# Two more Strassen products joined over two quarters, transposed spreads, a stacked rotary key and four-head value blocks in a two-layer encoder trunk

## The chip, the cores and the metric

The kernel runs on one core of a Trainium2 chip. The metric is device time in microseconds of one execution; a time given for a kernel is the median of several runs. A profile is one further execution, recorded by the hardware profiler. Engines are named as in the profile: PE (TensorE, matrix products), PEld (its weight loads), DVE (VectorE), ACT (ScalarE), POOL (GpSimd), SP (SyncE, which mainly issues DMAs).

## The reference

Input and output are 512 tokens of 1024 float32 features. Two layers work on a residual stream `h`. Between them one shared set of keys and values is computed.

```python
# layer 0
hn = rms_norm(h, mix_pre_g[0])
m  = conformer_conv(hn, ...)              # 1024->2048, gate, 31 taps, layer_norm, silu, 1024->1024
h  = h + rms_norm(m, mix_post_g[0])
f  = square(relu(rms_norm(h, ffn_pre_g[0]) @ w1)) @ w2    # 1024 -> 4096 -> 1024
h  = h + rms_norm(f, ffn_post_g[0])
# keys and values for layer 1
hn     = rms_norm(h, kv_in_g)
c_kv   = rms_norm(hn @ w_dkv, kv_norm_g)          # 256 wide
k_rope = apply_rope(hn @ w_kr, cos, sin)          # 64 wide, shared by the 8 heads
k_nope = c_kv @ w_uk                              # 8 heads x 128
v      = c_kv @ w_uv                              # 8 heads x 128
# layer 1
q  = rms_norm(rms_norm(h, mix_pre_g[1]) @ w_dq, q_norm_g) @ w_uq   # 8 x (128 + 64 rotary)
m  = attention(q, k_nope, k_rope, v, block-causal mask of 64 tokens) @ w_o
h  = h + rms_norm(m, mix_post_g[1])
f  = square(relu(rms_norm(h, ffn_pre_g[1]) @ w1)) @ w2
out = h + rms_norm(f, ffn_post_g[1])
```

## The kernel before

**Arithmetic.** A float32 operand `x` is held as two tiles of TensorE's fp32r type: `hi`, a ScalarE copy of `x`, and `lo = x - hi`, a VectorE subtraction. `split` makes the pair. A product is three fp32r products: hi by hi, lo by hi, hi by lo.

**A program that writes its own order.** `trunk` issues nothing directly. It records operations in a `Program`. `due` works backward and gives each one a latest time; `schedule` places them greedily on the engines, with modelled costs and, for DMAs, a modelled landing (`arrival`); `replay` runs the resulting order against a finer model of the DMA queues. `run` repeats due, schedule and replay 16 times, keeps the order with the shortest replayed span, and issues it. All instructions are issued from one line, L790, so the profile's groups differ by tile names and shapes and not by line. Where the schedule leaves TensorE empty, `schedule` adds filler products of the identity with itself (`mm<-ident` and `bc<-ident` in the profile).

**Tiles.** `big` is a pool of 49 tiles of 128x512 in SBUF. `tmp` has five more; `raw` (8) receives weights of 128x1024; `wh` (5) and `wl` (6) hold a weight's hi and lo parts; `mm` (6) and `bc` (2) are PSUM banks of 128x512; `stat` tiles hold a few numbers per token.

**Feed-forward.** The 4096 hidden features are taken in four quarters `q`. The first two use a Winograd form for the first matrix. In the third and fourth (`q` = 2 and 3) the block `ff1` computes eight products of 128 hidden features by 512 tokens, and ScalarE squares the rectified result into `Z`. The second matrix `ff2` is applied with Strassen's seven products over 2x2 blocks (token halves by hidden halves, hidden halves by output halves). Each of the seven is 24 products of 512 columns on TensorE: two halves `u` of the inner dimension, two token blocks `i`, two 128-wide slices and the three hi/lo combinations. `terms(p)` forms the left side (a difference of two `Z` blocks for products 1, 2, 5, 6 and 7) and splits it. `weight` forms the right side: a plain load on SP's queue, plus for products 3, 4, 6 and 7 an accumulating load on POOL's queue, or for product 1 a second plain load and a VectorE subtraction; then a split. `collect` adds a finished product to the accumulators, in the fourth quarter to every output block that it serves. After the third quarter the accumulators of the seven products are combined into the four output blocks.

Products 2 and 6 (`TOGETHER`) of the third quarter are not run there. Their left sides are kept as pairs, and they run at the end of the fourth quarter, into the same PSUM tiles as the fourth quarter's own products 2 and 6. The order `PRODUCTS` of the others is

```python
TOGETHER = (2, 6)
PRODUCTS = ((3, 6, 2, 1, 4, 5, 7),) * 2 + ((3, 1, 4, 5, 7), (3, 5, 1, 4, 7))
```

As output blocks become complete, `post_norm` takes them: square sums, the norm, the addition to `h`. In layer 0 it does so for tokens in two halves (`HA`, token blocks 0 and 1; `HB`, 2 and 3), and `prenorm` then transposes the half for the next layer on TensorE (`bc<-ident,h`). In layer 1 `finish` stores each token block in two halves, one from SP's queue and one from ScalarE's.

**Spreads.** `spread` turns a column of one number per token (`r`, in a `stat` tile) into a tile with that number along a row, the same in all 128 partitions: one float32 product of `r` broadcast with the identity per 128 tokens. There are four such blocks after the first norm, eight in the conv module's layer norm, four for the norm ahead of the keys (`r1`) and four in the key latents. `row_sums` multiplies by a constant matrix (`bc<-col,...`).

**Keys, queries, values.** For each half of the tokens, `latent` computes `c_kv` (2 x 24 products of 256 columns), then come the rotary key (`products(("kr",), ...)`, 24 products of 256 columns, its 64 columns twice side by side), `rotate` and two of the query latent's three blocks. The weights of `dkv`, `kr` and `dq` pass through `scaled`, which multiplies by a gain and splits. Then `project(u)` runs the up-projections listed in `PROJECTIONS` for the units `u` = -1 to 15, two per head, between the scores and the softmax of the heads. `values(pr)` makes the values of two heads: four token blocks of six products of 256 columns each.

Of the kernel before, what the change touches and what calls it, by code (L numbers as in the profile page):

```python
# [14 lines left out]
P = 128  # L15
# [21 lines left out]
for _name, _w in (  # L37
# [11 lines left out]


PROJECTIONS = {
    -1: (("uqr", 0), ("uq", 0), ("uq", 1), ("uk", 0), ("uk", 1), ("uv", 0)),
    0: (("uqr", 1),),
    1: (("uk", 2), ("uq", 2)),
    2: (("uv", 1),),
    3: (("uk", 3), ("uq", 3), ("uqr", 2)),
    5: (("uk", 4), ("uq", 4)),
    6: (("uv", 2),),
    7: (("uk", 5), ("uq", 5), ("uqr", 3)),
    9: (("uk", 6), ("uq", 6)),  # L60
    10: (("uv", 3),),
    11: (("uk", 7), ("uq", 7)),
}


# [11 lines left out]
}  # L77


TOGETHER = (2, 6)  # L80
PRODUCTS = ((3, 6, 2, 1, 4, 5, 7),) * 2 + ((3, 1, 4, 5, 7), (3, 5, 1, 4, 7))


BLK = {}
# [12 lines left out]
ATT = ("uq", "uqr", "uk", "uv", "wo")  # L97

GAINS = {"dq": "mix_pre1", "dkv": "kvin_g", "kr": "kvin_g"}


def _blk(name, cols=1024):
# [43 lines left out]
def _ff(layer):  # L146
    for q in EARLY:
        _first(layer, q)
    for q in range(4):
        for m in range(8 if q not in EARLY else 0):  # L150
            _blk(("ff1", layer, q, m))
        for dh in range(2):
            for ku in range(4):
                _blk(("ff2", layer, q, dh, ku))
                USE.pop()
        for r, p in [(q, p) for p in PRODUCTS[q]] + [(r, p) for r in (2, 3) for p in TOGETHER if q == 3]:
# [12 lines left out]
    _blk(("dq", _m))  # L169
for _u in range(-1, 16):  # L170
    for _key in PROJECTIONS.get(_u, ()):
        _blk(_key, {"uv": 512, "uqr": 384, "uq": 384, "uk": 256}[_key[0]])
_out("wo")
_ff(1)
NBLK = len(_cols)
# [108 lines left out]

BESIDE = 3000.0

FILL = 222.0

SLACK = 500.0
# [35 lines left out]
class Program:  # L325
# [14 lines left out]

    def record(self, *ways):
        op = Op(len(self.ops))
        op.early = self.early
# [96 lines left out]
        op.flight = 1500.0 + op.load + (3500.0 if slow > 1 else 0.0)  # L440

    def arrival(self, op, end, state):

        if "dma" not in op.method:
# [310 lines left out]
    def run(self, tags, rounds=16):  # L755
# [8 lines left out]
        for _ in range(rounds):  # L764
            self.due(start)
            span, start, sequence = self.schedule(tags)
            spans = [self.replay(sequence, pace) for pace in PACES]
# [26 lines left out]
def trunk(ctx: ExitStack, tc: tile.TileContext, xT, xN, wts, vec, along, rope, cw, out):  # L794
# [81 lines left out]
    def scaled(name, src):  # L876

        lo, hi = ([big(F32R) for _ in range(2)] for _ in range(2))
        for o in range(2):
# [153 lines left out]
    def spread(r, t0, n, dst=None, tag=BC):  # L1033

        bc = nc.tile(tag)
        for b in range(n // P):
            nc.tensor.matmul(
                bc[:, b * P : (b + 1) * P], lhsT=r[:, b : b + 1].to_broadcast([P, P]), rhs=ident, start=True, stop=True
            )
        if dst is not None:  # L1040
            nc.scalar.activation(dst[:, t0 : t0 + n], bc[:, :n], AF.Copy)
        return bc
# [219 lines left out]
    def feed_forward(layer, X, F):  # L1262
# [11 lines left out]
        for q in range(4):  # L1274
# [5 lines left out]
            for m in range(8 if q not in early else 0):  # L1280
# [3 lines left out]
                for th in range(2):  # L1284
# [4 lines left out]
            def terms(p):  # L1289

                left, A = STRASSEN[p][0], []
                for u in range(2):
                    src = Z[left[0][0]][u]
                    if len(left) > 1:
                        d = tmp()
                        nc.vector.tensor_tensor(out=d, in0=src, in1=Z[left[1][0]][u], op=ALU.subtract)
                        src = d
                    A.append(pair())
                    split(src, slice(0, T), A[u])
                return A  # L1300

            def sides(q, p):
                return [weight(("ff2", layer, q, p, u)) for u in range(2)]
# [31 lines left out]
                return b, to[1]  # L1335

            steps = [(u, i) for u in range(2) for i in range(2)]
            for p in PRODUCTS[q]:
                A = terms(p)
                collect(p, product({}, A, sides(q, p), steps))  # L1340
                if q == 3 and p in (5, 7):
                    for i in range(2):
                        yield done((0, int(p == 5)), i)
            if q > 1:
                for p in TOGETHER:
                    both[q, p] = terms(p)
            if q == 3:

                pts = {p: product({}, both[2, p], sides(2, p), steps, last=False) for p in TOGETHER}
                w = {p: sides(3, p) for p in TOGETHER}  # L1350
                for i in range(2):
                    for p in TOGETHER:
                        product(pts[p], both[3, p], w[p], [(0, i), (1, i)], first=False)
                        collect(p, {i: pts[p][i]})
                        yield done((1, int(p == 6)), i)
            if q == 2:

                for to, p in quad.items():
# [409 lines left out]
    def values(pr):  # L1768

        hi, lo = weight(("uv", pr))  # L1770
        V[pr] = [pair() for _ in range(2)]
        for tb in range(4):
            pt = nc.tile(MM)
            ts = slice(tb * P, (tb + 1) * P)
            for k in range(2):
                ws = slice(k * 256, (k + 1) * 256)
                for j, (a, b) in enumerate(((CKV[k][0], hi), (CKV[k][0], lo), (CKV[k][1], hi))):
                    nc.tensor.matmul(
                        pt[:, :256], lhsT=a[:, ts], rhs=b[:, ws],
                        start=(k == 0 and j == 0), stop=(k == 1 and j == 2),  # L1780
                    )
# [63 lines left out]
    def attend(hd, PT):  # L1845
        po = nc.tile(MM)
        seq = []
        for j, (n, o) in enumerate(((0, 0), (1, 0), (2, 0), (2, 2 * P))):
            vo = 256 * (j % 2) + 128 * (hd % 2)
            for a, b in ((0, 0), (0, 1), (1, 0)):  # L1850
                seq.append((j * P, V[hd // 2][j // 2][a][:, vo : vo + P], PT[n][b][:, o : o + T - j * P]))

        seq = seq[:1] + seq[3:] + seq[1:3]
        for n, (q0, a, b) in enumerate(seq):
# [47 lines left out]
def _layout(i):  # L1902
# [33 lines left out]
    put(("kr",), _tiles(np.concatenate([i["kv_w_kr"]] * 2, axis=1), slice(None)))  # L1936
    uq = i["mla_w_uq"][0].reshape(384, NH, 192)
    for p in range(4):
        put(("uv", p), _tiles(i["kv_w_uv"], slice(256 * p, 256 * (p + 1))))
# [80 lines left out]
```

## Time and profile before

| | |
|---|---|
| median of 3 runs | 1039.85 us (1039.79 to 1040.07) |
| profiled execution, own time | 1040.18 us |
| its span, first to last instruction | 1038.2 us |
| PE busy | 1024.0 us, 99% |
| DVE busy | 859.9 us, 83% |
| ACT busy | 676.0 us, 65% |
| POOL busy | 108.9 us, 10% |
| granted TensorE clock, mean | 0.996 |

How to read the profile: a group line names the operation, the tiles as out<-in without their numbers, and the shape; then the busy time, the mean duration of one in ns, and the idle time of the engine just ahead of them with what ended it. Matrix products overlap in their pipeline, so the mean duration of one is longer than the step from one to the next. In the order of time, equal neighbours are merged and counted (x72). A float32 product (not fp32r) leaves two records.

### The profile page before, as it was taken

To read this page: it belongs to the slowest core of one execution; us is meant where nothing else is said; L and a number is where in the kernel's file an instruction comes from. 1 tells how busy PE (TensorE), PEld (TensorE's weight loads), DVE (VectorE), ACT (ScalarE), POOL (GpSimd) and SP (SyncE) were. 2 spreads that over 40 slices of the span, in tenths; PEclk is the share of its full clock that TensorE was granted. 3 is DMA by queue.
4 is the path that set the end of the run, shared out by engine and by line. 5 is a ranking of instruction groups with operands and counts; after the bars stand their busy time and mean duration, and the time that the engine had idled before them with its cause. 6 is when DMAs were issued, how large, how long until landed. Compare 5 with 4: busy or idle time off the path is not lost.

```text
span 1038.2 us, 16186 instructions
## 1 busy us (share of the span) xinstructions
PE 1024.0 (99%) x5692; PEld 892.6 (86%) x5692; DVE 859.9 (83%) x1749; ACT 676.0 (65%) x1352; POOL 108.9 (10%) x148
## 2 busy tenths in 40 slices
PE   9999999999999999999999999999999999999996
PEld 7888988999988888888899888889998888888884
DVE  6998994997999648859989999549979995497798
ACT  8534895986876445465768777569767854455652
POOL 1113201102011010001000000010020111000010
PEclk9999999999999999999999999999999999999998
DMA  9985997558999977859422122936599999775782
GB/s 327 304 216 185 339 281 180 142 143 189 267 290 301 274 186 211 218 152 251 115 88 94 52 84 62 364 82 142 143 237 260 297 291 277 191 211 142 217 209 81
DMA packets 67217, 210.18 MB, mean 202 GB/s; under 512 B 8000, under 2 KB 11712, under 8 KB 67136
## 3 DMA queue, kind: packets, MB, share of 16 engines
q1 hardware_dynamic: 50112, 149.89, 41.3%
q0 software_dynamic: 16304, 58.20, 29.6%
q8 instruction: 45, 0.74, 0.3%
q10 hardware_dynamic: 720, 1.05, 0.3%
q14 instruction: 36, 0.29, 0.1%
HBM read 203.61 MB, written 5.51 MB: 201 GB/s over the span
## 4 chain that ended last, share of the span: by engine, by line
PE 82%; DVE 14%; ACT 2%; issue 1%; DMA 0%; DVEq 0%; ACTq 0%
PE mm L790 79%; DVE big L790 11%; PE bc L790 3%; DVE wl L790 1%; ACT big L790 1%; DVE tmp L790 1%; DVE stat L790 1%; DVE h L790 1%; ACT wh L790 1%; DMA vt<-vec 0%; ACT tmp L790 0%; ACT wl L790 0%; ACT junk L790 0%; DVE raw L790 0%; DVEq L2016 0%
## 5 line engine op out<-in xcount | busy, mean ns | idle before, releaser
L790 PE MATMUL mm<-big,wh 128*128 128x256 f32 (+1 forms) x1800 | 442.8, 336 | 0.4 <-ACT wh L790 0.4
L790 PE MATMUL mm<-wh,big 128*128 128x512 f32 (+1 forms) x1216 | 370.5, 385 | 0.0
L790 PEld LDWEIGHTS mm<-big,wh 128*128 128x128 f32 x1800 | 309.4, 190 | 34.6 <-ACT wh L790 1.3
L790 ACT ACTIVATE wh<-raw 128x512 fp32r<-128x512 f32 (+3 forms) x430 | 266.4, 661 | 103.3 <-PE mm L790 48.6
L790 PE MATMUL mm<-big,wl 128*128 128x256 f32 (+1 forms) x900 | 302.5, 336 | 0.0
L790 DVE TENSOR_TENSOR wl<-raw,wh 128x512 fp32r<-128x512 f32 (+3 forms) x366 | 248.0, 711 | 65.6 <-ACT wh L790 65.3
L790 PEld LDWEIGHTS mm<-wh,big 128*128 128x128 f32 x1216 | 225.9, 188 | 44.2 <-ACT wh L790 0.4
L790 PE MATMUL mm<-wl,big 128*128 128x512 f32 (+1 forms) x608 | 234.0, 386 | 0.0
L790 PEld LDWEIGHTS mm<-big,wl 128*128 128x128 f32 x900 | 171.4, 190 | 17.5 <-DVE wl L790 0.8
L790 DVE TENSOR_TENSOR big<-big,big 128x512 f32<-128x512 f32 (+4 forms) x216 | 126.7, 611 | 38.1 <-ACT big L790 27.4
L790 PEld LDWEIGHTS mm<-wl,big 128*128 128x128 f32 x608 | 114.2, 188 | 22.5 <-DVE wl L790 0.5
L790 PE MATMUL mm<-big,big 128*128 128x256 f32 (+10 forms) x840 | 118.5, 297 | 0.4 <-ACT big L790 0.4
L790 PEld LDWEIGHTS mm<-big,big 128*128 128x128 f32 x840 | 108.5, 191 | 4.9 <-ACT big L790 0.8
L790 POOL DMA_DIRECT2D raw<-wts x64 | 56.1, 896 | 430.1 <-DVE wl L790 126.2
L790 ACT ACTIVATE big<-big 128x512 f32<-128x512 f32 (+4 forms) x153 | 84.7, 573 | 14.4 <-DVE big L790 13.0
L790 ACT ACTIVATE big<-tmp 128x512 fp32r<-128x512 f32 (+2 forms) x152 | 75.0, 521 | 25.0 <-DVE tmp L790 24.0
L790 ACT ACTIVATE big<-mm 128x512 f32<-128x512 f32 (+5 forms) x126 | 64.9, 519 | 27.4 <-PE mm L790 26.5
L790 POOL DMA_DIRECT2D wl<-wts x42 | 36.6, 871 | 421.1 <-ACT wl L790 391.3
L790 DVE TENSOR_TENSOR big<-big,mm 128x512 f32<-128x512 f32 x102 | 66.9, 678 | 14.6 <-PE mm L790 14.4
L790 ACT ACTIVATE tmp<-mm 128x512 f32<-128x512 f32 (+1 forms) x41 | 25.0, 609 | 72.7 <-PE mm L790 69.9
L790 DVE SCALAR_TENSOR_TENSOR big<-big,vt,big 128x120 f32<-128x120 f32 (+30 forms) x105 | 67.3, 698 | 6.1 <-ACT big L790 5.9
L790 DVE TENSOR_TENSOR big<-tmp,big 128x512 fp32r<-128x512 f32 (+1 forms) x104 | 63.7, 622 | 4.5 <-ACT tmp L790 3.0
(87 smaller groups left out, 703.6 us busy)
## 6 DMA issues: line engine op xcount, KB each, us to landing
raw<-wts SPq DMA_DIRECT2D x224, 512.0 KB, 6.1
raw<-wts POOLq DMA_DIRECT2D x64, 512.0 KB, 8.6
wl<-wts POOLq DMA_DIRECT2D x42, 512.0 KB, 8.1
big<-cw SPq DMA_DIRECT2D x40, 256.0 KB, 8.8
big<-wts SPq DMA_DIRECT2D x12, 256.0 KB, 3.3
big<-along SPq DMA_DIRECT2D x10, 256.0 KB, 6.8
raw<-wts SPq DMA_DIRECT2D x12, 192.0 KB, 2.9
big<-xT SPq DMA_DIRECT2D x8, 256.0 KB, 4.2
```

The source lines that it names most:

```text
L790: return f(*args, **kwargs)
```

## The change

It has six parts.

1. Products 7 and 5 of the third quarter (`JOINT`) are treated like 2 and 6: they move to the fourth quarter, after its products 3, 1 and 4, and share PSUM tiles with its own products 7 and 5. A generator `finished` hands on an output block when every product that serves it has been collected.
2. The left sides that wait from the third to the fourth quarter are kept as whole float32 tiles (two per product, four products) and are split in the fourth quarter; before, they waited as pairs (four tiles per product, two products).
3. `spread` uses a transpose in place of the product with the identity, and so does the layout of the inverse norms `r1n`, whose row sums gave the same number.
4. The rotary key's weight is stacked: `hi` in the first 64 columns, `lo` in the other 64. One product gives hi by hi and lo by hi in the two halves of the partitions, a second of 64 columns adds hi by lo. The two halves are added with two ScalarE copies and one VectorE addition.
5. `values` makes four heads at a time, with products of 512 columns; the second block of four moves to unit 8.
6. In the program's own scheduling, a DMA's landing is no later than what the replay of the rounds before gave, plus 1000 ns. And `finish` stores with ScalarE's queue only for the second half of the last token block.

```diff
-    -1: (("uqr", 0), ("uq", 0), ("uq", 1), ("uk", 0), ("uk", 1), ("uv", 0)),
...
-    2: (("uv", 1),),
...
-    6: (("uv", 2),),
...
-    10: (("uv", 3),),
+    8: (('uv', 1),),

-TOGETHER = (2, 6)
-PRODUCTS = ((3, 6, 2, 1, 4, 5, 7),) * 2 + ((3, 1, 4, 5, 7), (3, 5, 1, 4, 7))
+JOINT, TOGETHER = (7, 5), (2, 6)
+WHOLE = (2, 6, 7, 5)
+PRODUCTS = ((3, 6, 2, 1, 4, 5, 7),) * 2 + ((3, 1, 4), (3, 1, 4))

+LATER, KEPT = 1000.0, 0.5
     def arrival(self, op, end, state):
+        there = self.modelled(op, end, state)
+        if "dma" in op.method and op.lasts is not None:
+            return min(there, end - op.cost + op.lasts + LATER)
+        return there

-            split(raw, slice(0, T), (hi[o], lo[o]))
+            if name[0] != "kr":
+                split(raw, slice(0, T), (hi[o], lo[o]))
+                continue
+            full, both, upper = (a.rearrange("p (k m) -> p k m", m=P) for a in (raw, hi[o], lo[o]))
+            nc.scalar.activation(both[:, :, :HALF], full[:, :, :HALF], AF.Copy)
+            nc.scalar.activation(upper[:, :, HALF:], full[:, :, HALF:], AF.Copy)
+            nc.vector.tensor_tensor(
+                out=both[:, :, HALF:], in0=full[:, :, HALF:], in1=upper[:, :, HALF:].bitcast(F32), op=ALU.subtract
+            )

+    def stacked_keys(t0, n):
+        w, _ = weight(("kr",))
+        pt = nc.tile(MM)
+        steps = [(0, 0)] + [(1, k) for k in range(KT)] + [(0, k) for k in range(1, KT)]
+        for i, (j, k) in enumerate(steps):
+            ks, m = k % 4 * P, (P, HALF)[j]
+            nc.tensor.matmul(
+                pt[:m, :n], lhsT=w[k // 4][:, ks : ks + m], rhs=XH[k][j][:, t0 : t0 + n],
+                start=(i == 0), stop=(i == len(steps) - 1),
+            )
+        s = slice(t0, t0 + n)
+        other, total = big(), big()
+        for j in range(2):
+            nc.scalar.activation(other[j * HALF : (j + 1) * HALF, s], pt[HALF - j * HALF : P - j * HALF, :n], AF.Copy)
+        nc.vector.tensor_tensor(out=total[:, s], in0=pt[:, :n], in1=other[:, s], op=ALU.add)
+        return total[:, s]

-            nc.tensor.matmul(
-                bc[:, b * P : (b + 1) * P], lhsT=r[:, b : b + 1].to_broadcast([P, P]), rhs=ident, start=True, stop=True
-            )
+            nc.tensor.transpose(bc[:, b * P : (b + 1) * P], r[:, b : b + 1].to_broadcast([P, P]), ident)

+            over = []
             for p in PRODUCTS[q]:
                 A = terms(p)
                 collect(p, product({}, A, sides(q, p), steps))
-                if q == 3 and p in (5, 7):
-                    for i in range(2):
-                        yield done((0, int(p == 5)), i)
-            if q > 1:
+                for i in range(2):
+                    yield from finished(p, i)
+            if q == 2:
+                for p in JOINT + TOGETHER:
+                    both[2, p] = left_sides(p, True) if p in WHOLE else terms(p)
+            if q == 3:
+                for p in WHOLE:
+                    both[2, p] = in_parts(both[2, p])
+                for p in JOINT:
+                    pts = product({}, both[2, p], sides(2, p), steps, last=False)
+                    collect(p, product(pts, terms(p), sides(3, p), steps, first=False))
                     for i in range(2):
+                        yield from finished(p, i)
                 for p in TOGETHER:
-                    both[q, p] = terms(p)
+                    both[3, p] = terms(p)
...
-        kr = dealt(rotate(products(("kr",), XH, *t), t[1], s, r1))[:, t[0] // M : (t[0] + t[1]) // M]
+        kr = dealt(rotate(stacked_keys(*t), t[1], s, r1))[:, t[0] // M : (t[0] + t[1]) // M]
...
-    nc.vector.tensor_copy(out=r, in_=row_sums([(b, r1n, b) for b in range(TB)], 0, D))
+    rt = nc.tile(BC)
+    for b in range(TB):
+        nc.tensor.transpose(rt[:, b * P : (b + 1) * P], r1n[:, b * P : (b + 1) * P], ident)
+    nc.vector.tensor_copy(out=r, in_=rt.rearrange("p (o k) -> p o k", k=P)[:, :, 0])
...
-        V[pr] = [pair() for _ in range(2)]
+        V[pr] = [pair() for _ in range(TB)]
...
-                        pt[:, :256], lhsT=a[:, ts], rhs=b[:, ws],
+                        pt, lhsT=a[:, ts], rhs=b[:, ws], start=(k == 0 and j == 0), stop=(k == 1 and j == 2)
...
-            split(pt, slice(0, 256), V[pr][tb // 2], slice(256 * (tb % 2), 256 * (tb % 2) + 256))
+            split(pt, ALL, V[pr][tb])
...
-            (nc.sync, nc.scalar)[cs.start > 0].dma_start(out=out[b, :, cs], in_=h[b][:, cs])
+            (nc.sync, nc.scalar)[b == TB - 1 and cs.start > 0].dma_start(out=out[b, :, cs], in_=h[b][:, cs])
```

More of the change, by code (lines that the diff above doesn't have):

```diff
@@ L51 @@
 PROJECTIONS = {
-    -1: (("uqr", 0), ("uq", 0), ("uq", 1), ("uk", 0), ("uk", 1), ("uv", 0)),
-    0: (("uqr", 1),),
-    1: (("uk", 2), ("uq", 2)),
-    2: (("uv", 1),),
-    3: (("uk", 3), ("uq", 3), ("uqr", 2)),
-    5: (("uk", 4), ("uq", 4)),
-    6: (("uv", 2),),
-    7: (("uk", 5), ("uq", 5), ("uqr", 3)),
-    9: (("uk", 6), ("uq", 6)),
-    10: (("uv", 3),),
-    11: (("uk", 7), ("uq", 7)),
+    -1: (('uqr', 0), ('uq', 0), ('uq', 1), ('uk', 0), ('uk', 1), ('uv', 0)),
+    0: (('uqr', 1),),
+    1: (('uk', 2), ('uq', 2)),
+    3: (('uk', 3), ('uq', 3), ('uqr', 2)),
+    5: (('uk', 4), ('uq', 4)),
+    7: (('uk', 5), ('uq', 5), ('uqr', 3)),
+    8: (('uv', 1),),
+    9: (('uk', 6), ('uq', 6)),
+    11: (('uk', 7), ('uq', 7)),
 }
@@ L99 @@
 GAINS = {"dq": "mix_pre1", "dkv": "kvin_g", "kr": "kvin_g"}
+HALF = P // 2
 def _blk(name, cols=1024):
@@ L155, in _ff @@
                 USE.pop()
-        for r, p in [(q, p) for p in PRODUCTS[q]] + [(r, p) for r in (2, 3) for p in TOGETHER if q == 3]:
+        for r, p in [(q, p) for p in PRODUCTS[q]] + ([(r, p) for p in JOINT for r in (2, 3)] + [(r, p) for r in (2, 3) for p in TOGETHER] if q == 3 else []):
             for u in range(2):
@@ L171 @@
     for _key in PROJECTIONS.get(_u, ()):
-        _blk(_key, {"uv": 512, "uqr": 384, "uq": 384, "uk": 256}[_key[0]])
+        _blk(_key, {"uv": 1024, "uqr": 384, "uq": 384, "uk": 256}[_key[0]])
 _out("wo")
@@ L342, in record @@
         op = Op(len(self.ops))
-        op.early = self.early
+        op.early, op.lasts = self.early, None
         self.ops.append(op)
@@ L442, in arrival, with modelled @@
     def arrival(self, op, end, state):
+        there = self.modelled(op, end, state)
+        if "dma" in op.method and op.lasts is not None:
+            return min(there, end - op.cost + op.lasts + LATER)
+        return there
+    def modelled(self, op, end, state):
         if "dma" not in op.method:
@@ L766, in run @@
             span, start, sequence = self.schedule(tags)
-            spans = [self.replay(sequence, pace) for pace in PACES]
+            spans, lasts = [], {}
+            for pace in PACES:
+                spans.append(self.replay(sequence, pace))
+                for op in self.ops:
+                    if "dma" in op.method:
+                        lasts[op] = max(lasts.get(op, 0.0), op.there - op.real)
+            for op, last in lasts.items():
+                op.lasts = last if op.lasts is None else KEPT * op.lasts + (1 - KEPT) * last
             span = sum(spans) / len(spans)
@@ L1288, in feed_forward, with left_sides @@
                     )
-            def terms(p):
-                left, A = STRASSEN[p][0], []
+            def left_sides(p, keep=False):
+                left, srcs = STRASSEN[p][0], []
                 for u in range(2):
@@ L1294, in terms, with in_parts @@
                     if len(left) > 1:
-                        d = tmp()
+                        d = big() if keep else tmp()
                         nc.vector.tensor_tensor(out=d, in0=src, in1=Z[left[1][0]][u], op=ALU.subtract)
                         src = d
+                    srcs.append(src)
+                return srcs
+            def in_parts(srcs):
+                A = []
+                for src in srcs:
                     A.append(pair())
-                    split(src, slice(0, T), A[u])
+                    split(src, slice(0, T), A[-1])
                 return A
+            def terms(p):
+                return in_parts(left_sides(p))
             def sides(q, p):
@@ L1337, in feed_forward, with finished @@
             steps = [(u, i) for u in range(2) for i in range(2)]
+            def finished(p, i):
+                if q == 3:
+                    over.append((p, i))
+                    for to, owner in quad.items():
+                        if to in STRASSEN[p][2] and all((o, i) in over for o in STRASSEN if to in STRASSEN[o][2]):
+                            yield done(to, i)
+            over = []
             for p in PRODUCTS[q]:
@@ L1340, in feed_forward @@
                 collect(p, product({}, A, sides(q, p), steps))
-                if q == 3 and p in (5, 7):
+                for i in range(2):
[3 more added lines that the diff above has]
+                    both[2, p] = left_sides(p, True) if p in WHOLE else terms(p)
+            if q == 3:
+                for p in WHOLE:
[3 more added lines that the diff above has]
+                    collect(p, product(pts, terms(p), sides(3, p), steps, first=False))
                     for i in range(2):
-                        yield done((0, int(p == 5)), i)
-            if q > 1:
+                        yield from finished(p, i)
                 for p in TOGETHER:
-                    both[q, p] = terms(p)
-            if q == 3:
+                    both[3, p] = terms(p)
                 pts = {p: product({}, both[2, p], sides(2, p), steps, last=False) for p in TOGETHER}
@@ L1354, in feed_forward @@
                         collect(p, {i: pts[p][i]})
-                        yield done((1, int(p == 6)), i)
+                        yield from finished(p, i)
             if q == 2:
@@ L1770, in values @@
         hi, lo = weight(("uv", pr))
-        V[pr] = [pair() for _ in range(2)]
-        for tb in range(4):
+        V[pr] = [pair() for _ in range(TB)]
+        for tb in range(TB):
             pt = nc.tile(MM)
@@ L1775, in values @@
             for k in range(2):
-                ws = slice(k * 256, (k + 1) * 256)
+                ws = slice(k * DH, (k + 1) * DH)
                 for j, (a, b) in enumerate(((CKV[k][0], hi), (CKV[k][0], lo), (CKV[k][1], hi))):
                     nc.tensor.matmul(
-                        pt[:, :256], lhsT=a[:, ts], rhs=b[:, ws],
-                        start=(k == 0 and j == 0), stop=(k == 1 and j == 2),
+                        pt, lhsT=a[:, ts], rhs=b[:, ws], start=(k == 0 and j == 0), stop=(k == 1 and j == 2)
                     )
-            split(pt, slice(0, 256), V[pr][tb // 2], slice(256 * (tb % 2), 256 * (tb % 2) + 256))
+            split(pt, ALL, V[pr][tb])
     def rotary(pr):
@@ L1848, in attend @@
         for j, (n, o) in enumerate(((0, 0), (1, 0), (2, 0), (2, 2 * P))):
-            vo = 256 * (j % 2) + 128 * (hd % 2)
+            vo = P * (hd % 4)
             for a, b in ((0, 0), (0, 1), (1, 0)):
-                seq.append((j * P, V[hd // 2][j // 2][a][:, vo : vo + P], PT[n][b][:, o : o + T - j * P]))
+                seq.append((j * P, V[hd // 4][j][a][:, vo : vo + P], PT[n][b][:, o : o + T - j * P]))
         seq = seq[:1] + seq[3:] + seq[1:3]
@@ L1938, in _layout @@
     for p in range(4):
-        put(("uv", p), _tiles(i["kv_w_uv"], slice(256 * p, 256 * (p + 1))))
+        if p < 2:
+            put(("uv", p), _tiles(i["kv_w_uv"], slice(512 * p, 512 * (p + 1))))
         rot = np.concatenate([uq[:, 2 * p, 128:], uq[:, 2 * p + 1, 128:]], axis=1)
```

## The prediction

> **What bounds the kernel now.** I read the page first, then the busy time by stage, then the groups of instructions by shape, then TensorE's order of time where the change works.
>
> ```profile
> span 1038.2 us, 16186 instructions
> PE 1024.0 (99%) x5692; PEld 892.6 (86%) x5692; DVE 859.9 (83%) x1749; ACT 676.0 (65%) x1352; POOL 108.9 (10%) x148
> ...
> q1 hardware_dynamic: 50112, 149.89, 41.3%
> q0 software_dynamic: 16304, 58.20, 29.6%
> ...
> PE 82%; DVE 14%; ACT 2%; issue 1%; DMA 0%; DVEq 0%; ACTq 0%
> ```
>
> TensorE is busy 99% of the span, so time is won by taking work from it or closing its few holes. The stages show the holes (columns: stretch; its length, then busy us of PE, PEld, DVE, ACT, POOL; clock, DMA share, GB/s):
>
> ```profile
> 0.00:10.00 10.00, 8.05 (x23) 5.93 (x24) 4.40 (x9) 7.48 (x15) 1.26 (x13) 1.00 0.79 257
> 10.00:132.60 122.60, 122.60 (x712) 107.89 (x712) 112.29 (x203) 74.39 (x151) 27.97 (x41) 1.00 0.91 275
> 132.60:142.00 9.40, 8.15 (x61) 7.23 (x60) 8.48 (x33) 7.40 (x15) 0.86 (x1) 1.00 1.05 305
> 142.00:438.00 296.00, 295.98 (x1652) 259.28 (x1651) 240.69 (x443) 201.82 (x384) 33.75 (x39) 1.00 0.81 221
> 438.00:462.00 24.00, 24.00 (x107) 19.87 (x107) 9.95 (x16) 12.65 (x28) 0.86 (x1) 1.00 0.52 142
> ...
> 470.00:502.00 32.00, 32.00 (x146) 26.51 (x145) 31.90 (x63) 20.64 (x44) 6.93 (x10) 1.00 1.00 253
> 502.00:515.20 13.20, 13.20 (x66) 11.02 (x64) 13.06 (x33) 7.51 (x19) 0.00 (x0) 1.00 0.18 52
> 515.20:531.00 15.80, 15.19 (x124) 14.43 (x123) 15.59 (x40) 11.96 (x32) 0.00 (x0) 1.00 0.25 78
> 531.00:660.00 129.00, 128.87 (x810) 114.98 (x809) 118.46 (x360) 97.16 (x220) 0.00 (x0) 1.00 0.31 103
> 660.00:1006.00 346.00, 346.00 (x1874) 300.94 (x1873) 268.81 (x465) 218.88 (x418) 36.37 (x42) 1.00 0.77 215
> ...
> 1028.00:1038.20 10.20, 0.00 (x1) 0.00 (x0) 6.44 (x23) 0.81 (x2) 0.00 (x0) 0.61 0.28 103
> ```
>
> The feed-forward stages are solid TensorE. It lacks work at the start, at the layer norm (132.6 to 142), where the first feed-forward hands over to the attention layer (515 to 531), and in the 10.2 us after its last product. From 470 to 531 VectorE is full too. Some of "busy" is filler: products of the identity that the program writes into predicted holes.
>
> **The change part by part.** The prices:
>
> ```profile
> L790 PE MATMUL bc<-ident,stat 128*128 128x128 f32 x32 | 4.8, 278 | 0.0
> L790 PE MATMUL mm<-ident,stat 128*128 128x128 f32 x8 | 1.3, 287 | 0.1
> L790 PE MATMUL bc<-ident,h 128*128 128x128 f32 x96 | 13.6, 275 | 0.3 <-DVE h L790 0.2
> L790 DVE TENSOR_TENSOR wl<-raw,wh 128x512 fp32r<-128x512 f32 x308 | 199.0, 683 | 54.7 <-ACT wh L790 54.5
> L790 DVE TENSOR_TENSOR big<-big,mm 128x512 f32<-128x512 f32 x102 | 66.9, 678 | 14.6 <-PE mm L790 14.4
> L790 DVE TENSOR_TENSOR big<-mm,big 128x256 fp32r<-128x256 f32 x16 | 6.3, 417 | 0.0
> L790 DVE TENSOR_TENSOR big<-mm,big 128x512 fp32r<-128x512 f32 x24 | 16.3, 684 | 2.9 <-ACT big L790 2.8
> ```
> ```profile
> 139.21 0.71 PE L790 MATMUL mm<-ident,stat 128*128 128x128 f32 x4
> 139.76 1.73 PE L790 MATMUL mm<-ident 128*128 128x128 f32 x14
> 141.24 0.47 PE L790 MATMUL mm<-wh,big 128*128 128x512 f32 x1
> ```
> ```profile
> 498.36 0.61 PE L790 MATMUL mm<-wh,big 128*128 128x512 f32 x2
> 498.81 0.39 PE L790 MATMUL mm<-wl,big 128*128 128x512 f32 x1
> 499.04 0.61 PE L790 MATMUL mm<-wh,big 128*128 128x512 f32 x2
> ...
> 503.15 0.40 PE L790 MATMUL mm<-wl,big 128*128 128x512 f32 x1
> 503.39 1.03 PE L790 MATMUL bc<-ident,h 128*128 128x128 f32 x8
> 504.18 0.71 PE L790 MATMUL mm<-wh,big 128*128 128x512 f32 x2
> ...
> 508.60 0.61 PE L790 MATMUL bc<-ident,stat 128*128 128x128 f32 x4
> 508.96 1.18 PE L790 MATMUL mm<-wh,big 128*128 128x512 f32 x4
> ...
> 515.20 8.79 PE L790 MATMUL mm<-big,big 128*128 128x256 f32 x72
> 523.83 2.17 PE L790 MATMUL bc<-ident 128*128 128x128 f32 x18
> 525.89 0.44 PE L790 MATMUL bc<-ident,h 128*128 128x128 f32 x2
> 526.56 0.88 PE L790 MATMUL bc<-ident,h 128*128 128x128 f32 x6 [0.23 <-DVE h L790]
> ...
> 557.00 1.05 PE L790 MATMUL bc<-col,big 128*128 128x128 f32 x8
> 557.81 0.48 PE L790 MATMUL mm<-big,wh 128*128 128x512 f32 x1
> ```
>
> TensorE's mean durations overlap; what an instruction costs is the step from start to start. 72 products of 256 columns take 515.20 to 523.83: 0.12 us each. Eight transposes hold the queue 503.39 to 504.18: 0.10 each. A 128-column f32 product is two records: four records (two blocks) take 508.60 to 508.96 and delay the next group by about 0.1, eight take 557.00 to 557.81, so some 0.11 a record, 0.22 a block. Three products of 512 columns take 498.36 to 499.04: 0.227 each.
>
> *Spreads as transposes.* 40 records (32 + 8) are 20 blocks; each becomes one transpose: 0.11 saved a block, 2.2 us in all. Not all is on the path. Four blocks serve the layer norm's first half, where 14 fillers (139.76 to 141.24) already cover a wait for VectorE: the saving there is only more filler. Two come just ahead of 515, where VectorE sets what follows. The other 14 (first norm 4, layer norm's second half 4, key and query stage 6) lie in solid TensorE: **1.55 us**.
>
> TensorE: Matmul & The Clock Gate, in the Trainium skill, says in its section Terms that trn2's transpose mode is four times faster for FP32. By that a block would cost 0.06 instead of 0.10, and this term would be 2.3 us. The trace disagrees: 96 transposes, eight of them in 0.79 us, stand at half of a product's price, so the rows decide.
>
> *The inverse norms by transposes.* The eight records at 557.00 become four transposes, 0.81 to about 0.4: **0.4 us**, in solid TensorE.
>
> *Stacked rotary key.* For each half of the tokens 24 products of 256 columns become 16; eight of them use 64 stationary columns. No row shows that form; I take 0.12, the price being that of the moving columns here, with 0.06 and 0.18 as ends. Each half saves 8 x 0.12 = 0.96. The second half's lies in solid TensorE: **0.95 us** (0.5 to 1.4). The first half's is the end of the run of 72 that ends at 523.83, and TensorE then fills until 525.89 because VectorE has not finished the second half's norm. Taking work from a cover buys nothing: 0 (up to 0.95 if something else fills the hole). Each half adds two ScalarE copies and a 256-wide VectorE add (0.42), and the weight's two VectorE splits shrink from 0.68 to about 0.42. The longer key path ends far ahead of the first scores: the query latents and the first projections come between.
>
> *Values of four heads.* 96 products of 256 become 48 of 512: 11.5 against 10.9: **0.6 us** (0 to 1.2). Evictions: 16 x 0.417 become 8 x 0.684 on VectorE, 1.2 us less, off the path. SP issues two weight loads instead of four, one of them earlier than half of its heads need it. Units 2, 6 and 10 lose 24 products (2.9 us) of cover each and four evictions (1.7 us); unit 8 gains 48 products' worth in one lump. VectorE is at 118.46 of 129.00 there. TensorE can pull the next projection forward, so I price this at nothing; without that cover it costs up to 3 x 1.2 = 3.6 us.
>
> *Products 7 and 5 joined.* In each layer they leave the third quarter and run in the fourth, into the same PSUM tiles as the fourth's own: the same 24 products each. Four VectorE adds of 0.68 a layer go (2.7 us), in the third quarter, where TensorE waits for nothing: 0. Into the fourth quarter move, per layer, 10.9 us of TensorE, eight 512-wide weight splits and four left splits, and four left splits of 2 and 6 that were done in the third quarter: 16 x 0.683 = 10.9 us of VectorE, as much as TensorE. So a VectorE that kept pace still does, just. Also moved: four loads on SP and two accumulating loads on POOL, past the fourth quarter's ff1 blocks and products 3, 1, 4 on both queues. The page prices them: 41.3% of the span for 149.89 MB is 1.50 us per 512 KB of plain load, 29.6% for 58.20 MB is 2.77 us of accumulating load. The fourth quarter's first five products (3, 5, 1, 4, 7) need 34.6 us of DMA in 27 us of TensorE; the new five (3, 1, 4, 7, 7) need 40.2. The loads must run 4 to 5 us further ahead. At 438 to 462 the DMA share is 0.52, so there is room: 0. If the lead isn't found: up to 4.3 us a layer. Tokens 0 and 1 now finish together after product 5, one product later than half of them did; the four joined products of 2 and 6 (22 us, 493 to 515) still cover them.
>
> *Output stores* of three blocks' second halves go from ScalarE's queue to SP's; the last block's pair, which ends the run, keeps its queues: 0. *Landings by the replay* changes only the order the program writes itself; it adds no work: 0, bounded by the holes, +/- 3 us.
>
> **Sum:** 1.55 + 0.4 + 0.95 + 0.6 = 3.5 us. The profiled execution takes 1040.18, 0.33 above the median: 1036.7, and **1036.3** for the median of 1039.85. If every term counted in full (2.2 + 0.4 + 1.9 + 0.6 = 5.1) it would be 1034.7.
>
> **Rivals.** *A, the hole closes too.* TensorE is without real work from 523.83 to 526.56, near 2.7 us, and 1.5 us of filler stand at 139.76. If the new order brings query products or an earlier second-half norm into the first, the 5.1 us count in full and some 2 to 3 more are won: about 1032. For: the hole is a matter of order. Against: VectorE is busy 15.59 of 15.80 there, and the joined products leave it as full. Chance 0.2.
>
> *B, the saving turns into waits.* With TensorE faster and VectorE at 92% in the attention stage and full from 470 to 531, two thirds of the 3.5 us reappear as waits: about 1038.6, no measurable change. For: the chain runs through VectorE for 14% of the span. Against: TensorE waits almost nowhere in 531 to 660. Chance 0.17.
>
> *C, the fourth quarter's products outrun their loads* (slower). DMA share is already 1.00 at 470 to 502. If a stall of 4.3 us comes in both layers: 1036.3 + 8.6 = 1044.9. It decides against the change from about 2.8 us a layer. Against: half-idle DMA right before. Chance 0.1.
>
> **How the numbers follow.** My forecast has 0.53, with its own range of 1034.7 to 1037.7. Against 1039.85, 0.2% is 2.1 us, about what a measurement of this kernel can tell from no change. Faster: forecast and A, 0.73. Same: B and the mild end of C, 0.18. Slower: 0.09. The range 1031.5 to 1040.5 leaves out most of C and the far end of A.
>
> **What would show it.** Spreads as 20 records and no longer 40; 64 products in place of 72 ahead of the hole, and a hole that opens about 1 us earlier and ends where it did relative to 515; VectorE's "big<-big,mm" 94 in place of 102; solid TensorE through the two fourth quarters. Wrong if TensorE shows waits there or in the attention stage, or if the time after the last product grows beyond 10.2 us.

## The result and the profile after

The changed kernel takes 1031.49 us (median; 1031.20 to 1031.78) against 1039.82 for the kernel before in the same comparison: a ratio of 0.9917, 95% interval 0.9905 to 0.9930, 8.3 us faster. The forecast was 1036.3 with a range from 1031.5. The direction was right, the size was not: the time is that of rival A, which had a chance of 0.2.

The page after:

```profile
span 1029.5 us, 15966 instructions
PE 1016.7 (99%) x5592; PEld 881.3 (86%) x5592; DVE 855.6 (83%) x1735; ACT 676.8 (66%) x1350; POOL 108.8 (11%) x148
```

TensorE is as full as before, over a span 8.7 us shorter, and 7.3 us less busy. Its groups after, and the VectorE adds of products:

```profile
L806 PE MATMUL mm<-ident 128*128 128x128 f32 x30 | 5.3, 339 | 1.6 <-POOL big L806 1.6
L806 PE MATMUL bc<-ident,stat 128*128 128x128 f32 x16 | 3.0, 276 | 0.0
L806 PE MATMUL mm<-big,big 128*64 128x256 f32 x16 | 2.7, 283 | 0.0
L806 PE MATMUL mm<-ident,stat 128*128 128x128 f32 x4 | 0.8, 284 | 0.0
L806 PE MATMUL bc<-ident 128*128 128x128 f32 x4 | 0.6, 275 | 0.0
...
L806 DVE TENSOR_TENSOR big<-big,mm 128x512 f32<-128x512 f32 x94 | 61.7, 679 | 8.4 <-PE mm L806 8.3
```

The 40 spread records are 20, the 102 adds are 94, and the 64-column products are there. The fillers named `bc<-ident` have fallen to 4; before, 18 stood in the hole at the hand-over alone. TensorE's order of time after, at the layer norm, then from the last product of layer 0's feed-forward to the second half's transposes, then at the end of the attention layer:

```profile
138.07 1.73 PE L806 MATMUL mm<-ident 128*128 128x128 f32 x14
139.55 0.48 PE L806 MATMUL mm<-wh,big 128*128 128x512 f32 x1
...
505.15 0.38 PE L806 MATMUL bc<-ident,stat 128*128 128x128 f32 x2
505.28 0.71 PE L806 MATMUL mm<-wh,big 128*128 128x512 f32 x2
...
513.09 6.84 PE L806 MATMUL mm<-big,big 128*128 128x256 f32 x56
519.76 0.38 PE L806 MATMUL bc<-ident,h 128*128 128x128 f32 x2
519.90 0.60 PE L806 MATMUL mm<-big,big 128*64 128x256 f32 x3
520.34 0.81 PE L806 MATMUL bc<-ident,h 128*128 128x128 f32 x6
520.91 2.54 PE L806 MATMUL mm<-big,big 128*128 128x256 f32 x17
523.72 1.06 PE L806 MATMUL bc<-ident,h 128*128 128x128 f32 x8 [0.26 <-DVE big L806]
524.53 2.54 PE L806 MATMUL mm<-big,big 128*128 128x256 f32 x19
...
687.07 0.38 PE L806 MATMUL bc<-ident,h 128*128 128x128 f32 x2
```

Of before, this row stands for the same last place:

```profile
695.00 0.38 PE L790 MATMUL bc<-ident,h 128*128 128x128 f32 x2
```

In the kernel before, the latents started at 515.20 and the second half's transposes came 10.7 us later (525.89), behind 18 fillers. Now they come 6.7 us later (513.09 to 519.76), and no filler stands between; the prediction had 64 products there and a hole behind them. Cut at these rows, the span divides so:

| stretch (us) | before | after | difference |
|---|---|---|---|
| start to the first product behind the layer norm (141.24; 139.55) | 141.24 | 139.55 | -1.7 |
| on to the start of the latents (515.20; 513.09) | 373.96 | 373.54 | -0.4 |
| on to the transposes behind the attention layer (695.00; 687.07) | 179.80 | 173.98 | **-5.8** |
| on to the end of the span (1038.2; 1029.5) | 343.2 | 342.4 | -0.8 |

Kernels that change nothing ahead of the layer norm differed from the kernel before by -0.2 to +0.7 us in the first stretch, so not all of its 1.7 us is won there. The third stretch is the case: its 5.8 us are most of the 8.7 that the span lost.

### The profile page after: what moved, and what is told of

It is laid out like the page before. It is cut to its first block, busy times and chain, and to the rows that moved or that the text cites. A ratio compares the mean times of both kernels' runs of the same rounds, so it can differ in the third digit from the quotient of the medians.

```text
span 1029.5 us, 15966 instructions
## 1 busy us (share of the span) xinstructions
PE 1016.7 (99%) x5592; PEld 881.3 (86%) x5592; DVE 855.6 (83%) x1735; ACT 676.8 (66%) x1350; POOL 108.8 (11%) x148
## 4 chain that ended last, share of the span: by engine, by line
PE 81%; DVE 12%; ACT 3%; issue 2%; DMA 1%; SPq 0%; DVEq 0%; ACTq 0%
PE mm L806 78%; DVE big L806 9%; PE bc L806 3%; DMA raw<-wts 1%; ACT big L806 1%; DVE wl L806 1%; DVE tmp L806 1%; ACT wh L806 1%; ACT tmp L806 0%; DVE stat L806 0%; ACT junk L806 0%; DVE h L806 0%; SPq L806 0%; DVE raw L806 0%; ACT wl L806 0%
## 5 line engine op out<-in xcount | busy, mean ns | idle before, releaser
L806 PE MATMUL mm<-wh,big 128*128 128x512 f32 x1184 | 369.4, 391 | 0.0
L806 PEld LDWEIGHTS mm<-wh,big 128*128 128x128 f32 x1184 | 221.7, 188 | 45.0
L806 PE MATMUL mm<-wl,big 128*128 128x512 f32 x592 | 231.0, 391 | 0.2 <-DVE wl L806 0.2
L806 DVE TENSOR_TENSOR big<-big,big 128x512 f32<-128x512 f32 (+4 forms) x250 | 146.2, 616 | 52.5 <-ACT big L806 41.2
L806 ACT ACTIVATE big<-big 128x512 fp32r<-128x512 f32 (+5 forms) x179 | 97.4, 566 | 10.7 <-DVE big L806 9.4
L806 ACT ACTIVATE big<-mm 128x512 f32<-128x512 f32 (+4 forms) x114 | 62.4, 551 | 22.4 <-PE mm L806 21.7
L806 DVE SCALAR_TENSOR_TENSOR big<-big,vt,big 128x120 f32<-128x120 f32 (+28 forms) x105 | 67.4, 714 | 5.9 <-ACT big L806 5.7
L806 ACT ACTIVATE big<-tmp 128x512 fp32r<-128x512 f32 (+2 forms) x136 | 65.8, 509 | 9.0 <-DVE tmp L806 6.0
L806 DVE TENSOR_TENSOR big<-big,mm 128x512 f32<-128x512 f32 x94 | 61.7, 679 | 8.4 <-PE mm L806 8.3
L806 DVE TENSOR_TENSOR big<-tmp,big 128x512 fp32r<-128x512 f32 (+1 forms) x88 | 52.6, 609 | 2.4 <-ACT tmp L806 2.4
```

Of the source, the lines that this page charges most:

```text
L806: return f(*args, **kwargs)
```

## The experiments

All are timed against the kernel before. First, the two parts that I had priced at nothing, each alone and each taken away. `joint_only` is the kernel before with:

```diff
-TOGETHER = (2, 6)
-PRODUCTS = ((3, 6, 2, 1, 4, 5, 7),) * 2 + ((3, 1, 4, 5, 7), (3, 5, 1, 4, 7))
+JOINT, TOGETHER = (7, 5), (2, 6)
+WHOLE = (2, 6, 7, 5)
+PRODUCTS = ((3, 6, 2, 1, 4, 5, 7),) * 2 + ((3, 1, 4), (3, 1, 4))
...
```

The left out lines are `left_sides`, `in_parts` and `finished`, as in the change.

> The kernel before with the joined products and whole left sides alone. Theory 1 (the joined products relieve VectorE: in the profile after, ten 512-wide splits of kept left sides stand in the fourth quarter's ff1 stage, and VectorE is less behind at the hand-over): the second half's transposes come 7 to 8 us after the start of the latents in place of 10.7, and the time falls by 2.5 to 4 us, to about 1036.5. Theory 2 (the landings let loads and weight splits run earlier): no change within 1 us, transposes still 10 to 11 us after. Theory 3 (the sum of TensorE's work, with nothing from order): no change within 0.5 us.

Measured: 0.9982 (0.9973 to 0.9991), 1.9 us faster; the transposes came 8.2 us after the latents' start. Theory 1 has the direction and about two thirds of the size. Of its ten splits one thing has to be set right: ten of that shape stand in the kernel after between 420.7 and 464, but its fourth quarter's ff1 stage is 407.22 to 450.74 and holds seven, where the stage before holds three.

`landings_only` is the kernel before with:

```diff
+        if "dma" in op.method and op.lasts is not None:
+            return min(there, end - op.cost + op.lasts + LATER)
```

> The kernel before with the landings by the replay alone. Theory 1: within 1 us of the kernel before, second half's transposes 10 to 11 us after the latents' start. Theory 2: 2.5 to 4 us faster, about 1036.5, transposes at 7 to 8 us, and DMA share in the fourth quarter's ff1 stage up from 0.5 to about 0.8. Theory 3: within 0.5 us.

Measured: 0.9987 (0.9978 to 0.9996), 1.4 us faster; transposes again 8.2 us after. So neither theory 1 nor theory 2 held alone: both parts shorten the same stretch. The loads did not fill the ff1 stage, though: DMA share there 0.63, where theory 2 had said 0.8. `all_but_joint` and `all_but_landings` are the changed kernel without the one and without the other of these two edits.

> The kernel after with products 7 and 5 and the left sides as before. Theory 1: 3 to 4 us slower than after, about 1035, and the hole before the second half's transposes is back with 10 to 11 us. Theory 2: within 1 us of after (1031.5), transposes at 7 us. Theory 3 (sum of work): about 1036 with or without the joined products.

Measured: 0.9944 (0.9931 to 0.9956), about 2.8 us behind the changed kernel, transposes 7.8 us after. The hole is back: 18 fillers, 2.1 us, stand ahead of them. The 10 to 11 us of theory 1 did not come, because the cover ahead of the fillers is now 48 products and no longer 72.

> The kernel after with the modelled landings of before. Theory 1: within 1.5 us of after (1031.5), transposes at 7 us. Theory 2: 3 to 4 us slower, about 1035, transposes at 10 to 11 us.

Measured: 0.9925 (0.9912 to 0.9939), 0.8 us behind by the ratios, which the intervals do not separate; transposes 7.6 us after, with 8 fillers in that stretch. Theory 2's 3 to 4 us did not come.

What the two parts do is seen on VectorE. For before, the two alone and the two together, the first row below is the fourth quarter's ff1 stage and the second its products up to the latents (columns as in the stages of the prediction; VectorE's busy time is the third that has a count in brackets, 28.20 in the first row). In order: before, `joint_only`, `landings_only`, `joint_and_landings`.

```profile
420.38:463.90 43.52, 43.52 (x193) 36.05 (x192) 28.20 (x47) 22.65 (x48) 2.59 (x3) 1.00 0.65 164
463.90:515.20 51.30, 51.30 (x238) 42.60 (x236) 51.06 (x105) 33.36 (x72) 7.80 (x11) 1.00 0.77 195
```
```profile
410.01:453.53 43.52, 43.52 (x194) 36.05 (x192) 29.63 (x50) 22.52 (x47) 4.32 (x5) 1.00 0.74 189
453.53:515.80 62.27, 62.27 (x285) 51.55 (x284) 61.62 (x122) 41.34 (x88) 7.80 (x11) 1.00 0.74 204
```
```profile
420.57:464.09 43.52, 43.52 (x194) 36.04 (x192) 30.02 (x50) 22.64 (x48) 3.46 (x4) 1.00 0.63 168
464.09:515.74 51.65, 51.56 (x237) 42.39 (x236) 51.04 (x104) 35.86 (x76) 6.96 (x10) 1.00 0.74 192
```
```profile
409.16:452.68 43.52, 43.52 (x193) 36.04 (x192) 31.00 (x52) 22.56 (x47) 4.81 (x6) 1.00 0.74 196
452.68:515.28 62.60, 62.47 (x286) 51.40 (x285) 61.70 (x122) 42.85 (x91) 7.28 (x11) 1.00 0.74 197
```

VectorE is full in the product stage in all four. The difference is how much it does ahead, in the ff1 stage where it has time: 28.2, 29.6, 30.0 and 31.0 us. With more done ahead, less is left for the hand-over, where the second half's norm stands in VectorE's queue: between the latents' start and the transposes VectorE is busy 10.52, 8.14, 8.14 and 6.81 us, nearly all of that stretch each time.

The next four take the terms of my sum one by one. `spreads_same_order` keeps the order of every queue as it was:

```diff
-            nc.tensor.matmul(bc[...], lhsT=r[:, b : b + 1].to_broadcast([P, P]), rhs=ident, start=True, stop=True)
+            nc.tensor.transpose(bc[...], r[:, b : b + 1].to_broadcast([P, P]), ident)
-            return 109.0 if method == "transpose" else ...
+            return 109.0 if method == "transpose" and list(ins[0].ap)[-1][0] else ...   # planned as before
```

> The kernel before with the 20 spread blocks as transposes, their planned cost left as it was, so that every engine's queue keeps exactly the order of before. Theory 3 (the sum): 1.5 to 2.2 us faster (14 to 20 blocks of 0.11). Theory 4 (a saving on TensorE that the order does not follow is given back at the next wait for VectorE): less than 1 us.

Measured: 0.9990 (0.9981 to 0.9998), 1.0 us. The interval, 0.2 to 2.0 us, holds values of both theories. Its layer norm shows the cover that the prediction had set four blocks aside for: the column is spread earlier, and the same 14 fillers follow.

```profile
138.38 0.43 PE L790 MATMUL mm<-ident,stat 128*128 128x128 f32 x2
138.65 1.73 PE L790 MATMUL mm<-ident 128*128 128x128 f32 x14
140.33 0.50 PE L790 MATMUL mm<-wh,big 128*128 128x512 f32 x1
```

The last two blocks start 1.95 us ahead of the first product (138.38 to 140.33) where it was 2.03 (139.21 to 141.24): some 0.2 us less work brings the product 0.08 nearer.

`spreads_only` has the same edit planned anew, and the inverse norms by transposes.

> The kernel before with the transposes (spreads and inverse norms) and the order planned anew. The sum says 2.0 us faster, 2.6 with every block; if a new order brings more, the first product behind the layer norm comes 1.5 us earlier than before and not 0.5.

Measured: 0.9990 (0.9981 to 0.9999), 1.0 us where the sum said 2.0. The first product behind the layer norm does come 1.5 us earlier, but the latents start only 0.6 earlier (514.57) and the second half's transposes 0.4 (525.53, behind 20 fillers). On the way TensorE waits for VectorE ahead of the first half's transposes, which the kernel before does not:

```profile
498.73 0.44 PE L790 MATMUL bc<-ident,h 128*128 128x128 f32 x2 [1.40 <-DVE h L790]
```

`key_only` (the stacked key's edits of the change) and `values_only` (the four-head values'):

> The kernel before with the stacked rotary key alone. The sum says 0.95 us faster (one half's eight products), 1.9 if the first half's count as well; the products with 64 stationary columns step by 0.12 us. Theory 4: nothing, the two halves' chains being set by VectorE.

Measured: 0.9982 (0.9974 to 0.9991), 1.9 us, twice the term. The row of its hand-over:

```profile
515.35 5.92 PE L791 MATMUL mm<-big,big 128*128 128x256 f32 x48
521.11 0.83 PE L791 MATMUL mm<-ident 128*128 128x128 f32 x6
521.73 1.67 PE L791 MATMUL mm<-big,big 128*128 128x256 f32 x12
525.18 0.41 PE L791 MATMUL bc<-ident,h 128*128 128x128 f32 x2 [1.78 <-DVE h L791]
```

The cover is shorter, as I had said, and TensorE waits; but the transposes come 9.8 us after the latents' start in place of 10.7. The norm itself was ready 0.9 us sooner, about the first half's 0.96. VectorE has less to do ahead of it, 9.73 us in place of 10.52: two of its splits there are now 256 wide, 0.42 each in place of 0.68, which is 0.5 of the 0.8.

> The kernel before with the values of four heads alone. The sum says 0.6 us faster; if units 2, 6 and 10 miss their cover, up to 3 us slower, with waits of TensorE in the attention stage that before does not have. If the 1.7 us that the attention stage lost in the kernel after come from VectorE's 1.2 us less, then 1.5 to 2 us faster.

Measured: 0.9991 (0.9982 to 1.0000), 0.9 us; the term was 0.6. One new wait of TensorE stands in its attention stage, 0.22 us for VectorE at 577.53.

Then the sum's parts together, and the two others together. `tensor_work_only` is the kernel before with spreads, inverse norms, stacked key and values; `joint_and_landings` with the other two parts.

> The kernel before with spreads, stacked key and four-head values: all that my sum counted, without joined products, landings and stores. My sum says 3.5 us faster (5.1 with every term in full). Adding up the three single runs (0.9990, 0.9982, 0.9991) says 0.9963, 3.8 us. If the parts help each other here, 5 us and more.

Measured: 0.9965 (0.9952 to 0.9977), 3.6 us. My sum was 3.5.

> The kernel before with joined products and landings, no TensorE work removed. If both only close the same hole ahead of the second half's transposes (each brought them from 10.7 to 8.2 us after the latents' start), together they give 2 to 2.5 us and the transposes at 7 to 8 us; if they add up, 0.9969, 3.2 us; if the rest of the gain of the kernel after (8.3 less 3.8) lies here, 4.5 us.

Measured: 0.9984 (0.9974 to 0.9993), 1.7 us; transposes 7.0 us after. The two close one hole, and the first of the three expectations is the nearest. Neither pair holds the missing 3 us (8.3 less 3.6 less 1.7; by the medians 8.3 less 4.1 less 2.1, 2.2 us). The hand-over of `tensor_work_only`:

```profile
513.82 5.92 PE L789 MATMUL mm<-big,big 128*128 128x256 f32 x48
519.57 3.74 PE L789 MATMUL bc<-ident 128*128 128x128 f32 x32
523.15 0.44 PE L789 MATMUL bc<-ident,h 128*128 128x128 f32 x2
```

and of `joint_and_landings`:

```profile
515.28 7.11 PE L808 MATMUL mm<-big,big 128*128 128x256 f32 x58
522.23 0.40 PE L808 MATMUL bc<-ident,h 128*128 128x128 f32 x2
```

With less work on TensorE and VectorE full as before (9.23 of the 9.33 us from the latents to the transposes), the hole has 32 fillers, 519.57 to 523.15, 3.6 us; before it had 18, 2.1 us. So 1.5 us of what TensorE saved became filler, and whatever relieves VectorE can win up to 3.6 us there and not 2.1.

`no_gain_products` asks directly whether VectorE sets the hole:

```diff
-            nc.vector.tensor_tensor(out=raw..., in0=raw..., in1=gain, op=ALU.mult)     # in scaled(), 12 times
```

> The kernel before without the twelve VectorE products that put the gains kv_in_g and mix_pre_g[1] into the weights of dkv, kr and dq (the gains are left out of the result). 12 x 0.686 = 8.2 us less VectorE work around the hand-over, TensorE's work unchanged. If VectorE sets the second half's transposes, they come 3 us and more earlier (at 7 to 8 us), and the time falls by 2.5 to 4 us. If something else sets them, no change within 1 us.

Measured: 0.9972 (0.9961 to 0.9983), 2.9 us, with TensorE's work untouched:

```profile
514.82 7.35 PE L790 MATMUL mm<-big,big 128*128 128x256 f32 x60
522.01 0.38 PE L790 MATMUL bc<-ident,h 128*128 128x128 f32 x2
```

7.2 us in place of 10.7, no filler. VectorE set it. `joint_as_pairs` asks what in the joined products relieves it (`WHOLE = ()`):

> joint_only with the four waiting left sides kept as pairs (16 big tiles in place of 8), split in the third quarter. If the gain of joint_only comes from the four adds a layer that are gone, 0.998 as there. If it comes from splits that fill VectorE's idle time in the fourth quarter's ff1 stage, VectorE is idle there again (3 to 4 of 10 us busy), the transposes come at 10 us, and the time is within 0.7 us of before.

Measured: 0.9990 (0.9982 to 0.9999), which the intervals don't separate from `joint_only`; the transposes came 8.2 us after, as there. But my expectation for VectorE failed: the ff1 stage was not idle again.

```profile
409.54:453.06 43.52, 43.52 (x194) 36.05 (x192) 31.77 (x53) 22.42 (x47) 4.94 (x6) 1.00 0.75 191
453.06:515.30 62.24, 62.24 (x286) 51.48 (x284) 58.27 (x116) 39.48 (x83) 7.21 (x11) 1.00 0.74 204
```

31.8 us of work were done there, and the program's own schedule had put the splits of the waiting sides among them:

```profile
418.64 0.68 DVE L791 TENSOR_TENSOR tmp<-big,big 128x512 f32<-128x512 f32 x1
419.24 0.68 DVE L791 TENSOR_TENSOR big<-tmp,big 128x512 fp32r<-128x512 f32 x1
...
428.03 1.29 DVE L791 TENSOR_TENSOR big<-tmp,big 128x512 fp32r<-128x512 f32 x2 [0.28 <-ACT big L791]
```

Five such subtractions and six such splits run from 418.64 to 429.32. The stage's eight blocks take 5.44 us each, so the first half of the hidden features is done at 431.3. Until then the fourth quarter has only one such left side that it could form, the first of product 6; the others need the second half, or block four. So at least five of the six splits belong to the sides that wait. The edit did not take the early splits away, and whether the gain needs them stays open, as it does for the adds that are gone and the room to prepare weights ahead. One thing it does show: VectorE did the most ahead of all these kernels, then had 4 us free in the product stage (58.27 busy of 62.24), and the transposes came no sooner than in `joint_only`. Work done ahead is not by itself what counts.

Last, whether hole and work together are the whole gain. `tensor_work_no_gains` is `tensor_work_only` with the edit of `no_gain_products`; `after_no_gains` is the changed kernel with that edit.

> tensor_work_only without the twelve gain products on VectorE (the gains are left out of the result); no joined products, no landings. Theory 5 (the extra of the kernel after is the hole at the hand-over: what TensorE saves ahead of it turns into filler there, 3.6 us in tensor_work_only, and whoever relieves VectorE gets both): the filler there is gone and the time is 7 to 8 us below before, ratio about 0.993, though the parts alone gave 3.6 and 2.9. Theory 6 (the joined products or the landings give something of their own elsewhere): the parts only add up, 6.5 us or less, 0.9938.

Measured: 0.9928 (0.9914 to 0.9942), 7.5 us, and

```profile
513.92 6.95 PE L789 MATMUL mm<-big,big 128*128 128x256 f32 x57
520.71 0.38 PE L789 MATMUL bc<-ident,h 128*128 128x128 f32 x2
```

no filler. That is in theory 5's window, but the whole time does not decide. Theory 6's bound of 0.9938 lies inside the interval, and the medians (4.1 and 3.2 us for the parts, 7.0 for both) and the profiles' spans (3.4, 3.4 and 6.9) are close to plain addition. The stretch itself speaks for theory 5. From the latents' start to the transposes behind the attention layer it is 179.80 us before, 178.09 in `tensor_work_only`, 176.97 in `no_gain_products` and 173.80 with both: 1.7, 2.8 and 6.0 us less. The two together win 1.5 us more than their sum, as much as the filler that `tensor_work_only` has more. Each of these is one profile; two kernels that should agree there, `joint_only` and `joint_as_pairs`, have 178.68 and 178.63.

> The kernel after without the twelve gain products (left out of the result). Theory 5: the hole is already closed in after, so 8.2 us less of VectorE work there give at most 1 us (TensorE's last waits there). If VectorE still set the hand-over, 2.5 us and more.

Measured: 0.9915 (0.9901 to 0.9929) beside the changed kernel's 0.9917. VectorE no longer sets the hand-over there: it is busy 4.72 of the 5.87 us from the latents to the transposes, and no more gain shows.

## Why the prediction was wrong, point by point

**The sum of TensorE's work** (3.5 us): right as a whole, 3.6 measured in `tensor_work_only`, but in part by luck: two errors of 1 us cancel. Spreads and inverse norms were sized 2.0 and gave 1.0 alone, with a new wait of 1.4 us for VectorE and two more fillers. The key was sized 0.95 and gave 1.9. Values: 0.6 against 0.9, within its interval. The price of a 64-column product, 0.12, held.

**The failed step** is the price 0 for the joined products ("so a VectorE that kept pace still does, just") and for the landings ("bounded by the holes"). I compared totals: 10.9 us of VectorE moved in, 10.9 us of TensorE moved in, so nothing changes. The total says nothing about when. VectorE was full in the product stage and had 15.3 us free in the ff1 stage just ahead (28.20 busy of 43.52), and both parts let it use more of that: 31.0 together, as the changed kernel's own rows also have it:

```profile
407.22:450.74 43.52, 43.52 (x193) 36.05 (x192) 30.99 (x52) 22.55 (x47) 5.18 (x6) 1.00 0.78 194
450.74:513.09 62.35, 62.22 (x284) 51.14 (x282) 61.46 (x121) 42.84 (x91) 6.90 (x10) 1.00 0.73 200
```

I had used that same room to argue that the loads would fit, and did not ask what it would do for VectorE. Without the joined products the changed kernel loses 2.8 us (`all_but_joint`), without the landings 0.8 (`all_but_landings`); in the third stretch the two lose 2.6 and 0.6 (176.59 and 174.58 against 173.98). With the stores, these parts are worth up to 4.7 us beside the others (8.3 less 3.6). That VectorE set the hole, and that these parts relieve it there, is shown; which piece of the joined products does it is not (`joint_as_pairs`). In layer 1 the price 0 was right: from the transposes at 695.00 to the end of the last product it is 333.0 us before, and 332.9 to 333.5 in the kernels with joined products.

**Terms set to nothing because they only shorten a cover** were right for the spreads alone, wrong for the key, whose first half counted even alone, and wrong for the change as a whole. Once the hole is closed, every term ahead of it counts in full. The third stretch fits that: the work taken out of it is 0.67 (six spread blocks), 0.4, 1.9 and 0.6, 3.6 us, and with the filler of 2.1 that makes 5.7; measured 5.8.

**Rival A** named the place, the size (5.1 and 2 to 3 more, 1032) and an earlier second-half norm as what closes the hole, and I held against it that "the joined products leave it as full". That sentence was the same mistake. That its number fits so well is in part luck: it did not hold the 1.2 us won behind the last product. **Rival B** is what happens to a part alone: it describes `spreads_only`, and `tensor_work_only` with its 32 fillers. **Rival C** did not come: TensorE is busy 62.22 of 62.35 us in the longer product stage, so loads and splits kept up but for 0.13 us.

**The price of a transpose.** Eight transposes take 523.72 to 524.53 after, 0.10 each, half of a float32 product's 0.22, as before. Two spread blocks delay the next product by 0.13 (505.15 to 505.28), where they delayed it by 0.36 (508.60 to 508.96): 0.11 saved a block, as priced. The factor of four in TensorE: Matmul & The Clock Gate, section Terms, in the Trainium skill, does not show in the eight. The rows were the right choice.

**The end of the span.** The time after the last product fell from 10.2 us to 9.0 and not beyond 10.2 as I had named for the wrong case:

```profile
1020.54:1029.50 8.96, 0.00 (x1) 0.00 (x0) 5.66 (x17) 0.81 (x2) 0.00 (x0) 0.77 0.31 117
```

VectorE has 5.66 us of work there where it had 6.44. Other kernels tell the two parts apart: this time is 9.8 to 10.3 us in those with neither joined products nor the new stores, 9.5 to 9.6 with the joined products alone, 9.6 with the stores alone (`all_but_joint`) and 9.0 to 9.2 with both. Each seems to give about half a microsecond, as much as the kernels with neither differ among themselves.

## What to carry to other kernels

Where two engines are both full at a hand-over, the gain of a change need not be the sum of its parts: work taken from the one can turn into waiting for the other, and relief of the other then wins that back too. Look for the filler or wait at that place, find which engine ends it, and price every part twice, with the hole open and with it closed. When work moves between stages, compare each engine's busy time stage by stage, not in total: an engine that is full in one stage may have free time in the stage just ahead.
